# One decoder layer: experts' rows each written to a place of their own and summed at the end, the last expert added on chip, per-layer work moved among the experts

## The chip, the cores and the metric

The program runs on one core of a Trainium2 chip. The metric is the device time of one execution in microseconds: the median of three runs of the kernel before is 1594.79 us (1594.51 to 1595.72). The profile shows one further execution. PE is the matrix engine, PEld its weight load, DVE, ACT and POOL the vector, scalar and general engines, SP the engine that here only issues DMAs.

## The reference, cut to what matters

One layer for 512 tokens of width 1024. Token mixing comes first (attention and a recurrent branch, merged and projected); it is untouched but for one set of stores. Then 32 experts, each token going to its best four, and last a gated per-layer input:

```python
xn = rmsnorm(h, norm_moe_g)
# per token: 4 of 32 experts, weights = softmax of the 4 best router logits
y_rows = (((clip(up) + 1) * swiglu(gate)) @ w_down[e] + b_down[e]) * weight
h = h + segment_sum(y_rows, token)          # four rows per token are added
pl_gate = sigmoid(rmsnorm(h, norm_pl_g) @ w_pl_gate + b_pl_gate)
pl = rmsnorm(p @ w_pl_proj, norm_pl_post_g)
out = rmsnorm(h + pl_gate * pl, norm_final_g)
```

Each expert has 12 MB of weights: `w_gate_up` 1024 x 2048 and `w_down` 1024 x 1024, in fp32. There are 2048 rows of results (512 tokens times 4) for 32 experts, 64 on average.

## The kernel before

**Weights.** All weights of the experts come through a ring of 20 buffers of 1 MB (`load_raw`, L622): eight of gate and up, four of down for each expert, 384 in all, issued by SP in that order. A buffer is loaded again as soon as PE has used it, so SP runs ahead of PE until it is short of buffers. Each hardware DMA uses one of eight semaphores in turn, so eight are outstanding.

**An expert.** The sorted order `ORDER` begins with two experts of the heavy class; then a light and a heavy one alternate, and the last two (numbers 30 and 31, counted from 0) are light. A heavy expert has room for 96 rows (three groups of 32), a light one for 64 (two). For each expert PE multiplies the gathered tokens with the eight gate-and-up buffers (`gate_up`, L924, an fp32 product for each group and quarter of the columns; four products on four column groups of the array run side by side, and each leaves two records in the trace), ACT and DVE apply the gating, and PE multiplies with the four down buffers (`down`, L974). ACT copies the result from PSUM with the row's weight (`h_t<-y,gate`).

**Adding up.** `scatter_add` (L893) adds the rows to the residual `h_dram` in HBM by an indirect DMA with an add, issued by POOL: 128 pieces of 512 numbers for the first 64 rows, and for a heavy expert 128 pieces of 256 numbers for the other 32. Places of an expert without a token go to rows of padding behind the 512 of `h_dram`. Each scatter waits for the one before.

**The end.** After the 384 weight buffers SP loads the per-layer projection `wpr`, the input `p` (`pt`) and the gate matrix (`pgr`). During the last expert PE transposes `pt` (L1067), after it PE computes the projection (`pp`, L1081 ff.; three products on rounded halves of the numbers, L70 to L72), and ACT and DVE split the gate matrix into halves (`pgh`, `pgl`). A branch (`tc.If`, L1094) follows that would compute further rows if an expert had more tokens than places; then `h_dram` is read back (`ht`, L1153). For each block of 128 tokens PE transposes `ht` (L1175) and multiplies with the gate matrix (`pg`, 48 products of 128x512), and DVE and ACT apply sigmoid, product, sum and the last norm.

Every engine works through its own list of instructions in order; the program's scheduler sets that list when the kernel is built, so a piece of code may stand earlier or later than in the text.

Of the kernel before, what the change touches and what calls it, by code (L numbers as in the profile page):

```python
# [20 lines left out]
P = 128  # L21
S = 512
# [20 lines left out]
def hybrid_block(  # L43
# [57 lines left out]
    mul2 = const.tile([P, 2], F32, name="mul2")  # L101
    off2 = const.tile([P, 2], F32, name="off2")
    pad2 = const.tile([P, 2], F32, name="pad2")
    for i, (n, m, s0) in enumerate(((64, 2, 0), (32, 4, 64))):
        part = const.tile([P, 2], I32, name=f"part{i}")
        nc.vector.tensor_single_scalar(part[:, 0:1], iota_p, n.bit_length() - 1, op=OP.logical_shift_right)
        nc.vector.tensor_single_scalar(part[:, 1:2], iota_p, n - 1, op=OP.bitwise_and)
        nc.vector.memset(mul2[:, i:i + 1], float(m))
        nc.vector.tensor_copy(off2[:, i:i + 1], part[:, 0:1])
        nc.vector.tensor_scalar(pad2[:, i:i + 1], part[:, 1:2], float(S + s0), float(m), op0=OP.add, op1=OP.mult)  # L110
    nc.vector.tensor_tensor(pad2, pad2, off2, op=OP.add)
# [28 lines left out]
    vals = route.tile([P, NTB, E, 5], BF16, name="vals")  # L140
# [6 lines left out]
    nc.vector.tensor_copy(vals[:, :, :, 3:], vidx.unsqueeze(2).to_broadcast([P, NTB, E, 2]))  # L147


    h_dram = dram.tile([S + CAP, D], F32, name="h_dram")  # L150
# [3 lines left out]
    vl_dram = dram.tile([P, E, NTB * 5], BF16, name="vl_dram")  # L154
# [10 lines left out]
    with ExitStack() as mix:  # L165
# [205 lines left out]
        with tc.tile_pool(name="s2", bufs=1) as s2, tc.tile_pool(name="p2", bufs=4, space=PSUM, reuse_waits="tile") as p2:  # L371
# [212 lines left out]
    LATE, NPL = 12 * E, 6  # L584

    def slot_of(n):
        return (n if n < LATE else n + NPL) % RING
# [6 lines left out]
    def raw_tile(n):  # L594
        return ring_tile(slot_of(n), [P, 2048], F32, f"raw{n}")
# [61 lines left out]
    def slot_rows(pool, psum, pe, vl, n=2):  # L657
# [3 lines left out]
        for i in range(n):  # L661
# [3 lines left out]
            for tb in range(NTB):  # L665
                nc.tensor.matmul(ip[:, i, :5], pes[i][:, tb], vl[:, tb], start=tb == 0, stop=tb == NTB - 1)
        iv = pool.tile([P, 2, 5], F32, name="ivg", bufs=2)[:, :n]
        act(iv, ip[:, :n, :5], AF.Copy)
# [5 lines left out]
        nc.vector.scalar_tensor_tensor(row, row, float(BIG), mul2[:, :n], op0=OP.add, op1=OP.mult)  # L674
        nc.vector.tensor_tensor(row, row, off2[:, :n], op=OP.add)
        dst = [pool.tile([P, 1], I32, name=f"dst{i}", bufs=2) for i in range(n)]
        for i in range(n):
            nc.vector.tensor_tensor(dst[i], row[:, i:i + 1], pad2[:, i:i + 1], op=OP.min)
# [6 lines left out]
    with ExitStack() as ep:  # L685
# [175 lines left out]
        for tb in range(NTB):  # L861
# [3 lines left out]
            nc.vector.tensor_reduce(gt[:, tb], oh.rearrange("q k e -> q e k"), axis=AX.X, op=OP.add)  # L865
    pjx.close()
# [5 lines left out]
    xpad = xp.tile([P, 128], F32, name="xpad")  # L872
# [16 lines left out]
    last_v = []  # L889
# [42 lines left out]
    def swiglu(psum, g, gu, aT):  # L932
# [6 lines left out]
        last_v.append(nc.vector.scalar_tensor_tensor(sg, sg, F7, u1, op0=OP.min, op1=OP.mult).ins)  # L939
# [12 lines left out]
    def down(psum, raws, aT, selcol, gate, y, rest, once=True, n=2):  # L952
# [19 lines left out]
        for i, k in order:  # L972
# [288 lines left out]
```

## Time and profile before

| | us |
|---|---|
| median of 3 runs | 1594.79 |
| profiled execution | 1593.8 |
| its span | 1592.2 |
| PE busy in the span | 1499.1 (94%) |
| DVE, ACT, POOL busy | 480.8, 422.8, 130.9 |
| share of the DMA engines: queue q1 (weights) | 71.8% |
| share of the DMA engines: queue q0 (POOL's DMAs) | 5.8% |

The experts take the stretch from 457 us to 1512 us. In the 40 slices of the page the DMA row reads 9 from slice 13 to slice 37 and the rate stands near 400 GB/s there; before it the DMA engines are mostly idle, and in the last three slices as well. A busy PE is not a PE at its peak: its share is read together with what it waits for.

### The profile page before, as it was taken

To read this page: it belongs to the slowest core of one execution; us is meant where nothing else is said; L and a number is where in the kernel's file an instruction comes from. 1 tells how busy PE (TensorE), PEld (TensorE's weight loads), DVE (VectorE), ACT (ScalarE), POOL (GpSimd) and SP (SyncE) were. 2 spreads that over 40 slices of the span, in tenths; PEclk is the share of its full clock that TensorE was granted. 3 is DMA by queue.
4 is the path that set the end of the run, shared out by engine and by line. 5 is a ranking of instruction groups with operands and counts; after the bars stand their busy time and mean duration, and the time that the engine had idled before them with its cause. 6 is when DMAs were issued, how large, how long until landed. Compare 5 with 4: busy or idle time off the path is not lost. (4 is left out here: it accounts for less than half of the span.)

```text
span 1592.2 us, 28449 instructions
## 1 busy us (share of the span) xinstructions
PE 1499.1 (94%) x11938; PEld 798.0 (50%) x11938; DVE 480.8 (30%) x1161; ACT 422.8 (27%) x764; POOL 130.9 (8%) x134
## 2 busy tenths in 40 slices
PE   7999999999999999999999999989999999999677
PEld 6888787777844343433434434334233332433256
DVE  7776655557432111211111111111121111210146
ACT  6878325555121110110111101011010110110167
POOL 1000000000001111101111011010110101101000
PEclk9999999999999999999999999999999999999889
DMA  7332431216788999999999999999999999999721
GB/s 221 98 106 80 123 102 54 80 57 235 288 344 328 371 395 401 398 393 392 397 400 390 396 402 396 392 393 399 401 396 402 389 397 403 398 400 398 310 80 53
DMA packets 105912, 479.99 MB, mean 301 GB/s; under 512 B 9857, under 2 KB 43353, under 8 KB 56016
## 3 DMA queue, kind: packets, MB, share of 16 engines
q1 hardware_dynamic: 93056, 450.97, 71.8%
q0 software_dynamic: 10448, 20.68, 5.8%
q10 hardware_dynamic: 2272, 6.45, 1.3%
q8 instruction: 95, 1.56, 0.4%
q14 instruction: 41, 0.34, 0.1%
HBM read 462.89 MB, written 17.17 MB: 302 GB/s over the span
## 5 line engine op out<-in xcount | busy, mean ns | idle before, releaser
L924 PE MATMUL gu<-raw,xa 128*32 128x512 f32 x5120 | 591.6, 594 | 24.6 <-DMA raw<-in_w_gate_up_dram 23.8
L924 PEld LDWEIGHTS gu<-raw,xa 128*32 128x32 f32 x5120 | 203.6, 110 | 364.9 <-issue 220.4
L974 PE MATMUL y<-raw,xa 128*32 128x512 f32 (+1 forms) x3072 | 316.7, 523 | 4.2 <-DMA raw<-in_w_down_dram 1.9
L937 DVE TENSOR_TENSOR sgu<-sgu,gu 128x256 f32<-128x256 f32 x48 | 20.2, 422 | 861.7 <-ACT sgu L62 861.7
L974 PEld LDWEIGHTS y<-raw,xa 128*32 128x32 f32 x3072 | 107.1, 109 | 158.0 <-issue 117.3
L62 ACT ACTIVATE sgu<-gu 128x256 f32<-128x256 f32 x48 | 18.4, 383 | 542.4 <-PE gu L924 542.4
L893 POOL DMA_INDIRECT h_dram<-h_t,dst x48 | 75.9, 1582 | 437.9 <-ACT h_t L62 298.4
L62 ACT ACTIVATE h_t<-y,gate 128x512 f32<-128x512 f32 (+1 forms) x48 | 29.6, 616 | 225.9 <-PE y L974 225.9
L62 ACT ACTIVATE whi<-wr 128x1024 fp32r<-128x1024 f32 x48 | 50.7, 1058 | 67.5 <-PE pj L71 36.8
L66 DVE TENSOR_TENSOR wlo<-wr,whi 128x1024 fp32r<-128x1024 f32 x47 | 57.2, 1219 | 26.0 <-ACT whi L62 25.7
L62 ACT ACTIVATE xa<-tpa 128x256 f32<-128x256 f32 x80 | 30.6, 383 | 123.0 <-PE tpa L947 99.3
L653 POOL TENSOR_SCALAR tok<-iv 64x1 int32<-64x1 f32 (+1 forms) x31 | 14.3, 461 | 500.6 <-ACT iv L62 500.6
L70 PE MATMUL pj<-xnh,whi 128*128 128x512 f32 x128 | 51.5, 403 | 0.0
L71 PE MATMUL pj<-xnl,whi 128*128 128x512 f32 x128 | 50.7, 396 | 0.0
L72 PE MATMUL pj<-xnh,wlo 128*128 128x512 f32 x128 | 50.2, 392 | 0.0
L917 PE MATMUL gu<-bias,eyep 96*32 96x512 bf16 x296 | 43.3, 384 | 5.6 <-DVE sgu L938 5.6
L62 ACT ACT_TABLE_LOAD x30 | 38.5, 1283 | 2.4 <-DVE lg L792 1.9
L636 POOL DMA_INDIRECT h_t<-xg_dram,tok x31 | 32.7, 1056 | 13.4 <-POOL tok L653 8.8
L947 PEld LDWEIGHTS tpa<-ident,sgu 128*128 128x128 f32 x96 | 15.1, 207 | 36.7 <-DVE sgu L939 23.3
L967 PE MATMUL y<-bias,eyep 96*32 96x512 bf16 (+1 forms) x176 | 20.1, 348 | 11.5 <-ACT h_t L62 11.5
L903 PE MATMUL tpx<-ident,h_t 64*128 64x64 f32 (+1 forms) x248 | 29.8, 245 | 0.8
L70 PE MATMUL pg<-pgh,hT 128*128 128x512 f32 (+1 forms) x72 | 26.9, 374 | 0.2 <-ACT hT L62 0.2
(366 smaller groups left out, 1954.4 us busy)
## 6 DMA issues: line engine op xcount, KB each, us to landing
raw<-in_w_gate_up_dram SPq DMA_DIRECT2D x256, 1024.0 KB, 22.0
raw<-in_w_down_dram SPq DMA_DIRECT2D x128, 1024.0 KB, 22.0
wr<-in_w_in_dram SPq DMA_DIRECT2D x12, 1024.0 KB, 5.3
wr<-in_w_merge_dram SPq DMA_DIRECT2D x8, 1024.0 KB, 5.5
wr<-in_w_lru_out_dram SPq DMA_DIRECT2D x4, 1024.0 KB, 5.1
wo<-in_w_out_dram SPq DMA_DIRECT2D x4, 1024.0 KB, 5.3
pgr<-in_w_pl_gate_dram SPq DMA_DIRECT2D x4, 1024.0 KB
xt<-in_x_dram SPq DMA_DIRECT2D x4, 512.0 KB, 6.1
```

The source lines that it names most:

```text
L62: return nc.scalar.activation(out_, in_, func, **kw).ins
L66: return eng.tensor_tensor(lo, src, hi.bitcast(F32), op=OP.subtract).ins
L70: nc.tensor.matmul(o, lh, rh, start=first, stop=False)
L71: nc.tensor.matmul(o, lh, rl, start=False, stop=False)
L72: nc.tensor.matmul(o, ll, rh, start=False, stop=last)
L636: return nc.gpsimd.indirect_dma_start(out=xr, out_offset=None, in_=xg_dram[:, :], in_offset=bass.IndirectOffsetOnAxis(ap=tok[:, 0:1], axis=0),
L893: nc.gpsimd.indirect_dma_start(out=h_dram.rearrange("r (c n) -> (r c) n", n=n), out_offset=bass.IndirectOffsetOnAxis(ap=dst[i][:, 0:1], ax ...
L903: nc.tensor.transpose(tp[:, j], xr[:cap, (j2 + j) * P:(j2 + j + 1) * P], ident[:cap, :cap])
L917: nc.tensor.matmul(gs[g][32 * j:32 * j + 32], selcol.to_broadcast([3 * E, 32]), src, start=True, stop=False)
L924: mm = nc.tensor.matmul(gs[g][32 * j:32 * j + 32], xT[:, k, 32 * g:32 * g + 32], src[:, :, 256 * j:256 * j + 256], start=False, stop=k == ...
L937: nc.vector.tensor_tensor(sg, sg, gp, op=OP.mult)
L974: mm = nc.tensor.matmul(o, aT[:, g, k % 2, k // 2], raws[k // 2][:, k % 2 * D + cs.start:k % 2 * D + cs.stop], start=False, stop=k == KT - ...
```

## The change

- **A place for each row.** A new tensor `y_dram` has four rows for each token. The column of the expert among the token's four (`kt`, carried as a sixth number in `vals`) gives the place, so no two rows meet, and `put` writes without an add. An expert's place without a token gets an index out of bounds and is dropped. `y_dram` is filled with zeros first: 16 stores of 0.5 MB on SP's queue, where one store of padding stood on ACT's.
- **Summing.** For each block of 128 tokens the four rows are read back (`planes`, two DMAs of 1 MB), and POOL (one) and DVE (three) add them to `h`.
- **The last expert** (number 31) isn't written: PE multiplies the one-hot matrix of its tokens with its result (`hp`, an fp32 product for each half of the columns) and DVE adds that.
- **Moved.** The projection's loads stand before expert 28's weights (two slots of the ring are kept for its result from there on), its product behind expert 28 (one fp32 product, `pl_product`, where three products of halves stood), its norm behind expert 29. The branch and the loads of the gate matrix, of the first block's rows and of `h` stand between the gate-and-up and the down buffers of expert 31; the split of the gate matrix stands within expert 31.

```diff
+    h_dram = dram.tile([S, D], F32, name="h_dram")
+
+    y_dram = dram.tile([S * TOPK, D], F32, name="y_dram")
...
+            zt = s2.tile([P, D], F32, name="zt")
             nc.gpsimd.memset(zt, 0.0)
-            nc.scalar.dma_start(h_dram[S:], zt)
+            for r in range(S * TOPK // P):
+                nc.sync.dma_start(y_dram[r * P:r * P + P], zt)
...
+    LATE, KEPT = 12 * (E - 4), 2
+    at_slot, turn = [], 0
+    for n in range(12 * E):
+        if n == LATE:
+            wpr_at, plt_at = turn % RING, [(turn + 1 + i) % RING for i in range(KEPT)]
+            turn += 1 + KEPT
+        while n >= LATE and turn % RING in plt_at:
+            turn += 1
+        at_slot.append(turn % RING)
+        turn += 1
...
+        nc.vector.tensor_scalar(row, row, float(BIG), float(TOPK), op0=OP.add, op1=OP.mult)
+        nc.vector.tensor_tensor(row, row, iv[:, :, 5], op=OP.add)
...
-    def scatter_add(y, dst):
+
+    def put(y, dst):
         for i, (a, n) in enumerate(((0, 512), (512, 256))[:len(dst)]):
             nc.gpsimd.indirect_dma_start(
-                out=h_dram.rearrange("r (c n) -> (r c) n", n=n),
+                out=y_dram.rearrange("r (c n) -> (r c) n", n=n),
                 out_offset=bass.IndirectOffsetOnAxis(ap=dst[i][:, 0:1], axis=0),
-                in_=y[:, a:a + n], in_offset=None, bounds_check=(S + CAP) * (D // n) - 1, oob_is_err=True,
-                compute_op=OP.add)
+                in_=y[:, a:a + n], in_offset=None, bounds_check=S * TOPK * (D // n) - 1, oob_is_err=False)
...
+        def load_rows(tb):
+
+            pr = [ring_tile(k, [P, 2, D], F32, "planes") for k in (DN[:2] if tb % 2 else FREE[4:])]
+            for i in range(2):
+                nc.sync.dma_start(pr[i], yv[tb * P:tb * P + P, 2 * i:2 * i + 2])
+            return pr
...
+        def tail_loads():
+
+            pgr = [ring_tile(k, [P, 2, D], F32, "pgr") for k in FREE[:4]]
+            for i in range(4):
+                nc.sync.dma_start(pgr[i], w_pl_gate[0].rearrange("(q i j) n -> i q j n", i=4, j=2)[i])
+            pr = [load_rows(0)]
+            h2 = [ring_tile(k, [P, 2, D], F32, "h2") for k in GU[:2]]
+            for i in range(2):
+                nc.sync.dma_start(h2[i], h_dram[i * 2 * P:(i + 1) * 2 * P].rearrange("(b t) d -> t b d", b=2))
+            return pgr, pr, h2
...
+        def pl_loads():
+
...
+            plts = [ring_tile(k, [P, 2, D], F32, "plt") for k in plt_at]
+            nc.sync.dma_start(wpr, w_pl_proj[0].rearrange("(k q) n -> q k n", q=P))
+            nc.sync.dma_start(pt, p[0, 0].rearrange("(b q) n -> q b n", q=P))
+            nc.sync.dma_start(gpl, norm_pl_g[0].rearrange("(q j) -> q j", j=KT))
...
+            for tb in range(NTB):
+                for n in range(2):
+                    ns = slice(n * 512, n * 512 + 512)
+                    pp = p_t.tile([P, 512], F32, name="pp7", tag="tp")
+                    for k in range(2):
+                        nc.tensor.matmul(pp, pT[:, tb, k], wpr[:, k, ns], start=k == 0, stop=k == 1)
+                    act(plts[tb // 2][:, tb % 2, ns], pp, AF.Copy)
+                    act(pp, pp, AF.Square, accum_out=sq[:, tb, n:n + 1])
+            return sq
...
+            if 12 * e == LATE:
+                wpr, pt, pT, gpl, plts = pl_loads()
+            raws = [load_raw(12 * e + t) for t in range(8)]
+            if e + 1 == E:
+                past()
+                pgr, pr, h2 = tail_loads()
+            raws += [load_raw(12 * e + t) for t in range(8, 12)]
...
+            else:
+
+                identb = fp.tile([P, P], BF16, name="identb", tag="pe")
+                nc.vector.tensor_copy(identb, ident)
+                tp = p_t.tile([P, S], F32, name="tpo", tag="tp")
+                for tb in range(NTB):
+                    nc.tensor.matmul(tp[:, tb * P:tb * P + P], pes[0][:, tb], identb, start=True, stop=True)
+                ohT = ob[:, 1, :S]
+                act(ohT, tp, AF.Copy)
+                whs, wls = tail_split()
...
-            split(wph[:, k], wpl[:, k], wpr[:, k])
-        for i in range(4):
...
+            if e + 1 < E:
+                put(y, dst)
+            if 12 * e == LATE:
+                sq = pl_product()
+            if 12 * e == LATE + 12:
+                ob = pl_norm()
...
+        def add_rows(tb, pr):
+            nc.gpsimd.tensor_tensor(pr[1][:, 0], pr[1][:, 0], pr[1][:, 1], op=OP.add)
+            nc.vector.tensor_tensor(pr[0][:, 0], pr[0][:, 0], pr[0][:, 1], op=OP.add)
+            nc.vector.tensor_tensor(ht[tb], ht[tb], pr[0][:, 0], op=OP.add)
+            nc.vector.tensor_tensor(ht[tb], ht[tb], pr[1][:, 0], op=OP.add)
+
+        def add_last(tb):
+
+            for c in range(2):
+                hp = ptl.tile([P, 512], F32, name="hp")
+                nc.tensor.matmul(hp, ohT[64 * c:64 * c + 64, tb * P:tb * P + P], y[64 * c:64 * c + 64, :512], start=True, stop=True)
+                nc.vector.tensor_tensor(ht[tb][:, c * 512:c * 512 + 512], ht[tb][:, c * 512:c * 512 + 512], hp, op=OP.add)
...
+        pr.append(load_rows(1))
+        add_rows(0, pr[0])
+        add_last(0)
...
         transpose_h(0)
         for tb in range(NTB):
-            act(junk, plt[tb], AF.Square, accum_out=sums[:, NTB + tb:NTB + tb + 1])
-        rsl = inv_rms(sums[:, NTB:])
-        for tb in range(NTB):
-            nc.vector.scalar_tensor_tensor(plt[tb], plt[tb], rsl[:, tb:tb + 1], gpo, op0=OP.mult, op1=OP.mult)
-        for tb in range(NTB):
             if tb + 1 < NTB:
+                add_rows(tb + 1, pr[tb + 1])
+                add_last(tb + 1)
+                if tb + 2 < NTB and tb + 2 == len(pr):
+                    pr.append(load_rows(tb + 2))
```

SP's list at the end of the experts, before (`raw_11570` is the last buffer of expert 31; a semaphore DMAHW is that of a load from SP, DMASW of a DMA from POOL):

```order
L622 DMA raw_11568<-in_w_down_dram 128x2048 [waits DMAHW2_49,PE_49]
L622 ISA
L622 DMA raw_11570<-in_w_down_dram 128x2048 [waits DMAHW3_49,PE_49]
L1038 DMA wpr<-in_w_pl_proj_dram 128x2x1024 [waits DMAHW4_49,PE_49]
L1039 DMA pt<-in_p_dram 128x4x256 [waits DMAHW5_49,PE_49]
L1044 DMA pgr_11578<-in_w_pl_gate_dram 128x2048 [waits DMAHW6_49,PE_49]
```

And after, from the last gate-and-up buffer of expert 31 over the branch; `raw_13335` is its first down buffer:

```order
L1101 DMA pgr<-in_w_pl_gate_dram 128x2048 [waits DMASW4_49,DMASW5_49,DMASW3_49,DMASW6_49,DMASW2_49,DMASW7_49,DMASW1_49,DMAHW2_49,DMASW0_49,PE_49]
L1101 DMA pgr<-in_w_pl_gate_dram 128x2048 [waits DMAHW3_49,DVE_49,Activation_49]
L1101 DMA pgr<-in_w_pl_gate_dram 128x2048 [waits DMASW7_49,DMAHW4_49,DMASW0_49,Activation_49]
L1101 DMA pgr<-in_w_pl_gate_dram 128x2048 [waits DMAHW5_49]
L1094 DMA planes<-y_dram 128x2048 [waits DMAHW6_49]
L1094 DMA planes<-y_dram 128x2048 [waits DMAHW7_49]
L1105 DMA h_13331<-h_dram 128x2x1024 [waits DMAHW0_49,PE_49]
L1105 DMA h_13332<-h_dram 128x2x1024 [waits DMAHW1_49,PE_49]
L626 ISA
L626 DMA raw_13335<-in_w_down_dram 128x2048 [waits DMAHW2_49]
```

Eight loads of 1 MB now stand ahead of the last four weight buffers, and the first of them waits for all of POOL's DMAs, the `put` of expert 30 among them.

PE's list at the end of expert 28 (a light expert; `y` is its down product, `gu` the next expert's gate and up) after the change; before, none of the rows `tpp` and `pp` stood here:

```order
L1141 MATMUL tpp<-ident,ptx 128x128 x4
L1148 MATMUL pp_11125<-wpr,ptx 128x512
L983 MATMUL y_11063<-raw_10930,xa 32x512 x8
L1148 MATMUL pp_11125<-wpr,ptx 128x512
L1148 MATMUL pp_11130<-wpr,ptx 128x512
L983 MATMUL y_11063<-raw_10932,xa 32x512 x8
L1148 MATMUL pp_11130<-wpr,ptx 128x512
L1148 MATMUL pp_11135<-wpr,ptx 128x512 x2
L1148 MATMUL pp_11140<-wpr,ptx 128x512 x2
L1148 MATMUL pp_11145<-wpr,ptx 128x512 x2
```

All 16 products of the projection and its eight transpositions stand between the down buffers of expert 28 and the next expert.

PE's list from expert 31's last down buffer on, before (`pp` is the projection):

```order
L974 MATMUL y_11723<-raw_11568,xa 32x512 x8
L974 MATMUL y_11723<-raw_11570,xa 32x512 x8
L72 MATMUL pp_11790<-wph,pT 128x512
L70 MATMUL pp_11798<-wph,pT 128x512
L71 MATMUL pp_11798<-wpl,pT 128x512
L72 MATMUL pp_11798<-wph,pT 128x512
```

And after:

```order
L983 MATMUL y_13478<-raw_13339,xa 32x512 x8
L983 MATMUL y_13478<-raw_13341,xa 32x512 x8
L1220 MATMUL hp<-h_t_3055,ob 128x512 x3
L1249 MATMUL tp_13551<-ident,h_13331 128x128 x4
L1249 MATMUL tp_13558<-ident,h_13331 128x128 x4
L1220 MATMUL hp<-h_t_3055,ob 128x512
L70 MATMUL pg_13602<-pgh,hT_13548 128x512
```

Behind the last down buffer PE now has the four `hp` of the first two blocks and eight transpositions before the gate product `pg`; the projection, the branch and the read of `h_dram` are gone from there.

## Rows read from the trace of the kernel before

**Rows 1.** Busy time by stretch: engines, granted clock, share of the DMA engines, rate.
```profile
680.00:932.60 252.60, 246.18 (x2360) 101.32 (x2360) 36.03 (x140) 28.11 (x76) 31.29 (x28) 1.00 1.02 396
932.60:1468.20 535.60, 500.26 (x4708) 190.03 (x4708) 71.05 (x277) 55.92 (x151) 60.81 (x54) 1.00 1.02 397
1535.20:1583.80 48.60, 48.38 (x240) 41.22 (x240) 31.90 (x57) 42.17 (x70) 0.00 (x0) 0.97 0.09 33
1583.80:1592.20 8.40, 0.00 (x0) 0.00 (x0) 2.95 (x10) 3.60 (x8) 0.00 (x0) 0.64 0.17 62
```
**Rows 2.** Longest wait of PE, first from 680 to 932.6, then from 932.6 to 1468.
```profile
PE y L967 <- ACT h_t L62: 3.4, 4, 0.8
...
PE gu L924 <- DMA raw<-in_w_gate_up_dram: 19.8, 31, 1.7
```
**Rows 3.** ACT's copy of experts' results (light experts): start, duration, instruction.
```profile
869.51 0.69 ACT L62 ACTIVATE h_t<-y,gate 128x512 f32<-128x512 f32 x1 [7.23 <-PE y L974]
...
932.64 0.69 ACT L62 ACTIVATE h_t<-y,gate 128x512 f32<-128x512 f32 x1 [7.23 <-PE y L974]
...
1402.93 0.69 ACT L62 ACTIVATE h_t<-y,gate 128x512 f32<-128x512 f32 x1 [9.37 <-PE y L974]
...
1468.24 0.69 ACT L62 ACTIVATE h_t<-y,gate 128x512 f32<-128x512 f32 x1 [7.23 <-PE y L974]
```
**Rows 4.** DMA queue q0, 1470 to 1479 us, one scatter of 256 KB: packets, MB, share.
```profile
q0 software_dynamic: 144, 0.26, 15.8%
```
**Rows 5.** DMA queue q0, 1450 to 1460 us, one scatter of 128 KB.
```profile
q0 software_dynamic: 144, 0.13, 8.2%
```
**Rows 6.** DMA queue q1, 1566 to 1574 us, two stores of the output, 256 KB each.
```profile
q1 hardware_dynamic: 288, 0.52, 17.7%
```
**Rows 7.** DMA issues of the whole run: count, KB each, median us to landing.
```profile
wr<-in_w_in_dram SPq DMA_DIRECT2D x12, 1024.0 KB, 5.3
...
h_dram<-h_t,dst POOLq DMA_INDIRECT x48, 9.1
```
**Rows 8.** DMA issues, 1513 to 1520 us: the last scatter, with little other traffic.
```profile
h_dram<-h_t,dst POOLq DMA_INDIRECT x1, 5.0
```
**Rows 9.** Timeline, expert 30's gate and up at the pace of its loads.
```profile
1449.84 1.92 PE L924 MATMUL gu<-raw,xa 128*32 128x512 f32 x16 [0.50 <-DMA raw<-in_w_gate_up_dram]
...
1452.34 1.92 PE L924 MATMUL gu<-raw,xa 128*32 128x512 f32 x16 [0.58 <-DMA raw<-in_w_gate_up_dram]
```
**Rows 10.** Timeline from the last expert's down product to the first gate product.
```profile
1500.57 1.54 PE L1067 MATMUL tpp<-ident,pt 128*128 128x128 f32 x6 [9.09 <-DMA pt<-in_p_dram]
...
1504.87 7.07 PE L974 MATMUL y<-raw,xa 128*32 128x512 f32 x62
...
1512.04 0.69 ACT L62 ACTIVATE h_t<-y,gate 128x512 f32<-128x512 f32 x1 [7.45 <-PE y L974]
1512.62 8.41 ACT L62 ACTIVATE pgh<-pgr,gpl 128x1024 fp32r<-128x1024 f32 x8
1513.19 1.57 POOL L893 DMA_INDIRECT h_dram<-h_t,dst  x1 [42.44 <-ACT h_t L62]
...
1535.22 0.80 PE L70 MATMUL pg<-pgh,hT 128*128 128x512 f32 x1 [0.24 <-ACT hT L62]
```
**Rows 11.** Chain of waits in order of time: one gate product in the dense stretch.
```profile
1560.14 0.23 PE pg L71
```
**Rows 12.** Groups by line: mean duration of passes over 128x1024 fp32.
```profile
L66 DVE TENSOR_TENSOR wlo<-wr,whi 128x1024 fp32r<-128x1024 f32 x47 | 57.2, 1219 | 26.0 <-ACT whi L62 25.7
...
L66 POOL TENSOR_TENSOR wlo<-wr,whi 128x1024 fp32r<-128x1024 f32 x1 | 2.4, 2387 | 13.2 <-ACT whi L62 13.2
...
L1196 DVE SCALAR_TENSOR_TENSOR plt<-plt,rs,rows 128x1024 f32<-128x1024 f32 x4 | 4.9, 1281 | 0.0
```
**Rows 13.** DMA queue q10, 180 to 200 us: stores of padding and loads of biases.
```profile
q10 hardware_dynamic: 160, 0.52, 8.2%
```
**Rows 14.** ACT, rounding of the projection `v`, first and second piece.
```profile
198.61 1.15 ACT L62 ACTIVATE vwh<-wr 128x512 fp32r<-128x512 f32 x2 [4.38 <-PE yp L71]
204.05 1.16 ACT L62 ACTIVATE vwh<-wr 128x512 fp32r<-128x512 f32 x2 [4.29 <-PE yp L71]
```

More of the change, by code (lines that the diff above doesn't have):

```diff
@@ L98, in hybrid_block @@
     nc.gpsimd.iota(iota_p, pattern=[[0, 1]], base=0, channel_multiplier=1)
-    mul2 = const.tile([P, 2], F32, name="mul2")
     off2 = const.tile([P, 2], F32, name="off2")
[L103 to L111, printed above, removed]
+    for i, n in enumerate((64, 32)):
+        part = const.tile([P, 1], I32, name=f"part{i}")
+        nc.vector.tensor_single_scalar(part, iota_p, n.bit_length() - 1, op=OP.logical_shift_right)
+        nc.vector.tensor_copy(off2[:, i:i + 1], part)
     trib = const.tile([P, P], BF16, name="trib")
@@ new lines, in tail_split @@
+        def tail_split():
+            whs = [ring_tile(k, [P, 2, D], F32R, "pgh") for k in GU[4:]]
+            wls = []
+            for i in range(4):
+                wls.append(ring_tile([GU[2], *FREE][i], [P, 2, D], F32R, "pgl"))
+                for j in range(2):
+                    gc = gpl[:, 2 * i + j:2 * i + j + 1]
+                    act(whs[i][:, j], pgr[i][:, j], AF.Copy, scale=gc)
+                    nc.vector.scalar_tensor_tensor(wls[i][:, j], pgr[i][:, j], gc, whs[i][:, j].bitcast(F32),
+                                                   op0=OP.mult, op1=OP.subtract)
+            return whs, wls
@@ new lines, in pl_norm @@
+        def pl_norm():
+            ob = r1.tile([P, 2, D], F32, name="ob", tag="a8b")
+            nc.sync.dma_start(ob[:, 0], norm_pl_post_g[0:1].to_broadcast([P, D]))
+            rsl = fp.tile([P, NTB], F32, name="rsl")
+            nc.vector.tensor_tensor(rsl, sq[:, :, 0], sq[:, :, 1], op=OP.add)
+            act(rsl, rsl, AF.Sqrt, scale=1.0 / D, bias=eps)
+            nc.vector.reciprocal(rsl, rsl)
+            for tb in range(NTB):
+                pl = plts[tb // 2][:, tb % 2]
+                nc.vector.scalar_tensor_tensor(pl, pl, rsl[:, tb:tb + 1], ob[:, 0], op0=OP.mult, op1=OP.mult)
+            return ob
@@ L1083, in hybrid_block @@
-        for tb in range(NTB):
-            for n in range(2):
-                ns = slice(n * 512, n * 512 + 512)
-                pp = p_gu.tile([P, 512], F32, name="pp7", tag=f"gu{(2 * tb + n) % G}")
-                for k in range(2):
-                    mm3(pp, (pT[:, tb, 0, k], pT[:, tb, 1, k]), (wph[:, k, ns], wpl[:, k, ns]),
-                        first=k == 0, last=k == 1)
-                act(plts[tb // 2][:, tb % 2, ns], pp, AF.Copy)
-    cnt = nc.values_load(cm_i[0:1, 0:1], min_val=0, max_val=S)
@@ L1146, in hybrid_block @@
+            down(p_y, raws[8:], aT, sel, gate, y, rest, n=n)
+            if e + 1 < E:
+                put(y, dst)
+            if 12 * e == LATE:
+                sq = pl_product()
+            if 12 * e == LATE + 12:
+                ob = pl_norm()
+            if e + 2 == E:
+                nc.vector.tensor_copy(cm_i, cmax)
     with tc.tile_pool(name="tl", bufs=2, reuse_waits="tile") as tl, \
             tc.tile_pool(name="ptl", bufs=2, space=PSUM, reuse_waits="tile") as ptl:
-        rows = [spare(n, [P, 2, D], F32, f"rows{n}") for n in (17, 18)]
```

213 lines of the change are left out of this document (92 added, 121 removed).

## The prediction

> **What bounds the kernel now.** I read the stretches of the page first, then the waits of PE, then the times at which experts' results are copied, and last the timeline of the end. In the experts' stretch the share of the DMA engines is 1.02 from 680 to 1468 us, at 396 to 397 GB/s [rows 1]: it is full all the time. PE is not always short of data, though. From 680 to 932.6 us it never waits for a weight buffer, from 932.6 on it does [rows 2]. The copies of light experts show the same: one pair (a heavy and a light expert) takes 63.13 us early (869.51 to 932.64), and 535.6 / 8 = 66.95 us later (932.64 to 1468.24, eight pairs) [rows 3]. So 63.1 us per pair is PE's own pace, 66.95 that of the transfers, and PE lives on a full ring until about 935 us. From there the experts end when the transfers do. Behind them comes a serial end: PE waits 9 us for `pt`, finishes expert 31, its result is copied at 1512.04, and the first gate product starts at 1535.22, 23.2 us later, with 8.41 us of ACT's splitting in between [rows 10]. Then PE is busy 48.38 of 48.6 us, and 8.4 us follow without PE [rows 1].
>
> **Scatter without add.** One add of 256 KB takes 0.158 x 9 = 1.42 us of all DMA engines [rows 4], one of 128 KB 0.082 x 10 = 0.82 us [rows 5]. There are 48 [rows 7]: 32 of the first kind and 16 of the second (heavy experts), 32 x 1.42 + 16 x 0.82 = 58.6 us. What a plain write costs is shown by the output: two stores of 256 KB in the same 2 KB packets take 0.177 x 8 = 1.42 us, so 0.71 us each, half [rows 6]. That gives 31 x 0.71 + 16 x 0.41 = 28.6 us, and if places without a token cost nothing (2048 rows in 32 x 64 + 16 x 32 = 2560 places), 0.8 times that, 22.9 us. Saved: 30 to 36 us; I take 33. The bounds are 36 and nothing (a write in the crowd costs what an add does), and I lean on the output's row because its packets are of the same size.
>
> 33 us over 16 pairs is 2.1 per pair, 66.95 - 2.1 = 64.9 us: nearly PE's pace. By transfers the copy of expert 28 (1402.93 before) comes at 1402.93 - 33 x 28/32 + 3.8 = 1377.8, where 3.8 us are the 1.5 MB of `wpr` and `pt` now ahead of it at 2.5 us per MB (two waits for a buffer lie 2.50 us apart [rows 9]). By PE it comes at 932.64 + 7 x 63.13 = 1374.6. I take 1378, so from here PE sets the pace.
>
> **Zero stores.** Eight MB on SP's queue ahead of the second load for `v`. In the stores of the padding 0.52 MB took 0.082 x 20 = 1.64 us of all engines [rows 13], so 8.4 MB take 26 us from about 174 us, and the load behind them lands near 206 instead of before 199. Its rounding is due at 199, PE wants the result at about 204 [rows 14]. Cost 0 to 8 us, I take 2, since PE has the group before to work on. Everything later shifts: 1380. The routing's few added passes lie beside PE's products and cost nothing here; without that cover, some 4 us.
>
> **Projection behind expert 28.** 16 fp32 products of 128x512. Sixteen records of the experts' product take 1.92 us, four column groups side by side, two records to a product [rows 9], so a product on the full array takes 0.86 us here by estimate, and 16 take 13.8; eight transpositions (six in 1.54 us when cold, L1067 [rows 10]) about 0.9. Together 14.7 us of PE. The lower bound is 16 x 0.23 = 3.7 [rows 11]; I take the upper, as these are not split into halves. PE has just caught up with the transfers, so nothing hides it: expert 30 is one pair later, 1380 + 14.7 + 63.1 = 1457.8.
>
> **The new wait.** SP's first `pgr` load waits for the `put` of expert 30, and behind it stand all four `pgr`, two `planes`, two `h` and the last four down buffers: 12 MB. POOL issues the `put` about 1.1 us behind the copy (1513.19 against 1512.04 [rows 10]); it lands 5.0 us after that when quiet [rows 8], 9.1 in the crowd [rows 7]. I take 7, since the loads of expert 31's gate and up end by then: 1466. In this gap of some 7 us the transfers have nothing to do. The first MB lands 5.3 us after issue from a quiet queue [rows 7], eleven more follow at 2.5: 1466 + 5.3 + 27.5 = 1498.8. Expert 31's gate and up (13.7 us of PE), the split of `pgr` and the adding of the first rows lie in that time and cost nothing; the branch too.
>
> **The end.** The last buffer takes 1.9 us of PE, the copy 0.8: 1501.5, against 1512.73 before. Then two `hp`, an add, a third `hp` before the transpositions, these, their copy and the fourth: two products of 0.86, 0.8 for the add, then 2 for transpositions and copy, in all 4.6: the first gate product starts at 1506.1 instead of 1535.2. The dense stretch of 48.6 grows by four more `hp` (3.4) and 1 us of small waits, then 8.4 follow: 1506.1 + 48.6 + 3.4 + 1 + 8.4 = 1567.5. The profiled execution took 1593.8 at a span of 1592.2, so 1.6 lie around it: 1569.1, 24.7 below its own time. The median of the runs is 1.0 above the profiled one: **1570 us**.
>
> In that end DVE does 31.90 + 2.95 - 4.9 = 30 us for four blocks [rows 1, 12], 7.5 each. Added are three passes of 1.22 and two of half that, 4.9: 12.4 us per block, against PE's 48 x 0.23 + 0.9 + 1.7 = 13.6. PE stays ahead by about a us.
>
> **Rivals.**
> - *DVE sets the end.* POOL's added pass takes 2.39 us where DVE's takes 1.22 [rows 12], and no row shows both at once on 1024 columns. If DVE stands still for POOL's three passes in the dense stretch, its block takes 14.8 instead of 12.4 and is longer than PE's: 3 x 1.2 + 2.4 for the first block's start, 6 us, 1576. For: the margin is one us. Against: DVE can begin block 0 before PE. The Trainium skill (GPSIMD Engine Reference, section 1, Specifications) says that the two engines share their interfaces to SBUF and that DVE's instructions with two SBUF inputs contend, which speaks for this rival; no run here shows it yet.
> - *PE's time for the projection is partly hidden*, the `put` lands in 5 us and the zeros cost nothing: 4 + 2 + 2 less and small waits gone, near 1560; with the projection wholly hidden, 1555. For: if transfers are slower than I think, PE has waits to fill behind expert 28, and its products stand between two down buffers. Against: then the saving is smaller as well.
> - *No gain.* A write in the crowd costs nearly what an add costs, saving 8 instead of 33 us: 25 x 28/32 = 22 later, 1592. Most of the shortened end is then paid for by the 8 MB now ahead of the last weights. For: reads and writes share the engines, and the output's row is from a quiet stretch. Against: the adds were read in the crowd and cost twice as much at the same size.
> - *Slower.* The mechanism is the same price, further on: `put` pieces of 2 KB and 1 KB, each to a row of its own, cost as much as the adds or more. Saving nothing puts expert 30 at 1457.8 + 29, and the 12 MB queue behind its `put`: 1599. It decides from a price of 1.4 us for 256 KB at all places, or 1.75 if empty places are free. The stores of the output [rows 6] speak against it.
>
> A rule that would help and not hurt: the Trainium skill (Runtime: NRT & Kernel Launch, section Instruction fetch mechanics) says a taken branch whose target lies outside the current pages stalls its engine for the fetch. The branch left PE's path at the end for a place where PE waits anyway; by that rule a few us of the 23.2 go with it, and they are already in my sum, which counts the new end from its own parts.
>
> **How the numbers follow.** Forecast (1562 to 1582) 0.58, DVE sets the end 0.14 (mostly inside that range's upper part), hidden projection 0.12, no gain 0.09, slower 0.07. A difference of 0.2% (3 us) is what a measurement of this kernel tells from none. Of the case without gain a third each falls faster, within and slower: faster 0.87, within 0.2% 0.04, slower 0.09. Range 1553 to 1590: from the hidden projection with the saving of 36, to the forecast with a saving of about 12 (21 x 28/32 = 18 later). The likeliest one's own range is 1562 to 1582; cases of the other sign hold little.
>
> **What would show it.** Right: pairs of experts at 63 to 65 us up to expert 28; no wait of PE for weights before 1300 us; a pair behind expert 28 with about 15 us of `pp`; DMA engines idle for 5 to 10 us around 1460, ended by the `put`; the last down buffer near 1499; first `pg` within 8 us of it; `pg` dense for 52 us. A scatter of 256 KB at 0.5 to 0.75 us of all engines. Wrong: pairs still at 67 us (the price of a write), PE waiting for DVE's `hT` or adds in the dense stretch by more than 3 us, a gap in PE near 204 us above 4, or an end of the experts that comes 15 us later than 1499.

## The result, and the profile after

The changed kernel takes 1578.64 us (median of four runs, 1577.56 to 1579.38) where the one before takes 1595.09 in the same series: a ratio of 0.9896, interval 0.9879 to 0.9913. It is 16.5 us faster; I had forecast 1570, 24.8 faster. The profiled execution has a span of 1576.6 us.

Busy time by stretch of the changed kernel (PE, PEld, DVE, ACT, POOL, then the granted clock, the share of the DMA engines and GB/s); the first and the last line answer to those of [rows 1]:

```profile
680.00:932.60 252.60, 246.20 (x2364) 101.02 (x2360) 35.91 (x140) 28.11 (x76) 24.51 (x28) 1.00 1.02 407
932.60:1314.80 382.20, 371.90 (x3562) 151.05 (x3555) 53.87 (x210) 42.17 (x114) 36.77 (x42) 1.00 1.01 404
1380.00:1420.00 40.00, 40.00 (x261) 13.09 (x258) 3.46 (x10) 14.27 (x31) 1.02 (x1) 1.00 0.71 276
...
1418.00:1504.40 86.40, 65.37 (x604) 21.28 (x594) 28.52 (x57) 15.91 (x30) 7.76 (x6) 0.88 1.01 411
1512.80:1568.90 56.10, 53.03 (x249) 42.37 (x248) 44.08 (x65) 34.33 (x58) 7.41 (x3) 0.94 0.23 86
```

The third line is new: from 1380 to 1420 us the DMA engines move 276 GB/s instead of about 410 while PE is busy all the time. Before that they are full and after it they are full again, to the last weight buffer.

ACT's copies of light experts, as in [rows 3], and of the last expert:

```profile
935.08 0.69 ACT L62 ACTIVATE h_t<-y,gate 128x512 f32<-128x512 f32 x1 [7.23 <-PE y L983]
...
1314.82 0.69 ACT L62 ACTIVATE h_t<-y,gate 128x512 f32<-128x512 f32 x1 [7.23 <-PE y L983]
...
1387.37 0.69 ACT L62 ACTIVATE h_t<-y,gate 128x512 f32<-128x512 f32 x1 [1.55 <-PE y L983]
...
1459.78 0.69 ACT L62 ACTIVATE h_t<-y,gate 128x512 f32<-128x512 f32 x1 [7.23 <-PE y L983]
...
1506.95 0.69 ACT L62 ACTIVATE h_t<-y,gate 128x512 f32<-128x512 f32 x1 [19.28 <-PE y L983]
```

Six pairs from 935.08 to 1314.82 are 63.29 us each: PE's pace now holds to 1314 us, where it gave way to the transfers' 66.95 at 933 before. The two pairs that share the projection take 72.55 and 72.41.

The loads' queue `q1` and POOL's queue `q0` from 935 to 1315 us (packets, MB, time as a share of 16 engines), with SP's issues of weight buffers in that stretch (behind the x their number; the kernel before also shows the median us to landing), first in the kernel before, then after the change:

```profile
q1 hardware_dynamic: 19737, 143.72, 93.5%
q0 software_dynamic: 3520, 6.59, 8.0%
...
raw<-in_w_gate_up_dram SPq DMA_DIRECT2D x89, 1024.0 KB, 22.4
raw<-in_w_down_dram SPq DMA_DIRECT2D x47, 1024.0 KB, 23.1
```

```profile
q1 hardware_dynamic: 20231, 147.31, 96.2%
q0 software_dynamic: 2400, 6.06, 4.7%
...
raw<-in_w_gate_up_dram SPq DMA_DIRECT2D x95, 1024.0 KB
raw<-in_w_down_dram SPq DMA_DIRECT2D x44, 1024.0 KB
```

In 380 us POOL's queue takes 30.4 us for 5.7 pairs before and 17.9 for 6.0 after: 5.4 and 3.0 us per pair. The loads move 2.5% more, so their own pace is now 66.95 x 143.72 / 147.31 = 65.3 us per pair, by estimate. That is slower than PE's 63.29: SP issued 139 weight buffers while PE used the 144 of six pairs. PE drew on the lead that the full ring had given it, and at expert 28 it had to wait for six buffers (PE's waits from 1310 to 1390 us, the first row):

```profile
PE gu L933 <- DMA raw<-in_w_gate_up_dram: 4.1, 6, 0.9
```

One `put` of up to 256 KB, that of expert 30, from 1460 to 1472 us:

```profile
q0 software_dynamic: 80, 0.22, 4.7%
```

It took 0.047 x 12 = 0.56 us of all DMA engines, where an add took 1.42 [rows 4].

What SP waits for from 1370 to 1480 us in the changed kernel (total, times, longest):

```profile
SPq L626 <- PE pp L1148: 23.5, 1, 23.5
...
SPq L1101 <- DMA h_t<-xg_dram,tok: 11.5, 1, 11.5
```

The first wait is one load of expert weights whose slot of the ring still holds `wpr`: it can only go once the last product of the projection has read it. While SP stands there the transfers run dry. The second is the wait of the first `pgr` load for POOL's DMAs; the `put` of expert 30, issued at 1460.74, landed 8.2 us later, at 1468.9, and the load went out at 1471.12. The row names one of POOL's gathers as the last to release it, and what held it for those last 2 us is open.

The timeline of the end, from the last expert's down product to the first gate product, answers to [rows 10]:

```profile
1497.46 6.90 PE L983 MATMUL y<-raw,xa 128*32 128x512 f32 x48 [12.88 <-DMA raw<-in_w_down_dram]
1504.96 1.92 PE L983 MATMUL y<-raw,xa 128*32 128x512 f32 x16 [0.60 <-DMA raw<-in_w_down_dram]
...
1507.69 1.13 PE L1220 MATMUL hp<-h_t,ob 64*128 64x512 f32 x4 [0.81 <-ACT h_t L62]
...
1510.65 1.16 PE L1249 MATMUL tp<-ident,h 128*128 128x128 f32 x8
...
1512.79 0.50 PE L70 MATMUL pg<-pgh,hT 128*128 128x512 f32 x1
```

From copy to first gate product it is 5.8 us instead of 23.2. But the rest, 48.6 + 8.4 us before, is 63.8 now (1512.8 to 1576.6), and in it PE waits once for DVE:

```profile
PE tp L1249 <- DVE h L1221: 3.1, 1, 3.1
```

DVE and POOL just ahead of that wait; each stretched pass of DVE lies beside one of POOL (L1211):

```profile
1512.58 2.40 POOL L1211 TENSOR_TENSOR planes<-planes 128x1024 f32<-128x1024 f32 x1 [19.24 <-DMA planes<-y_dram]
1513.24 2.82 DVE L1213 TENSOR_TENSOR h<-h,planes 128x1024 f32<-128x1024 f32 x1
...
1517.52 2.38 POOL L1211 TENSOR_TENSOR planes<-planes 128x1024 f32<-128x1024 f32 x1 [2.54 <-DMA planes<-y_dram]
1518.61 2.38 DVE L1212 TENSOR_TENSOR planes<-planes 128x1024 f32<-128x1024 f32 x1
1522.77 1.21 DVE L1213 TENSOR_TENSOR h<-h,planes 128x1024 f32<-128x1024 f32 x1
...
1524.67 2.85 POOL L1211 TENSOR_TENSOR planes<-planes 128x1024 f32<-128x1024 f32 x1 [4.77 <-DMA planes<-y_dram]
1525.21 2.87 DVE L1291 TENSOR_TENSOR gs<-gs,plt 128x512 f32<-128x512 f32 x1
```

PE's clock around that wait, in the changed kernel (columns as above):

```profile
1525.00:1530.00 5.00, 4.37 (x18) 2.66 (x17) 5.00 (x6) 0.35 (x2) 2.53 (x1) 1.00 0.00 0
1530.00:1532.40 2.40, 0.00 (x0) 0.00 (x0) 2.40 (x6) 2.37 (x4) 0.00 (x0) 0.77 0.00 0
1532.40:1538.40 6.00, 5.95 (x19) 5.02 (x20) 5.27 (x7) 5.04 (x10) 0.00 (x0) 0.52 0.00 0
```

After the 3.1 us without work the granted clock is 0.52 for 6 us, which is nearly all at the lower of the two levels, 1.2 GHz: some 3 us more are lost than the wait itself.

### The profile page after: what moved, and what is told of

Read it like the earlier page. It is cut to its first block, busy times and chain, and to the rows that moved or that the text cites. A ratio compares the mean times of both kernels' runs of the same rounds, so it can differ in the third digit from the quotient of the medians.

```text
span 1576.6 us, 28522 instructions
## 1 busy us (share of the span) xinstructions
PE 1503.3 (95%) x11954; PEld 802.8 (51%) x11954; DVE 506.8 (32%) x1188; ACT 420.3 (27%) x766; POOL 113.7 (7%) x137
## 5 line engine op out<-in xcount | busy, mean ns | idle before, releaser
L933 PE MATMUL gu<-raw,xa 128*32 128x512 f32 x5120 | 585.1, 594 | 5.0 <-DMA raw<-in_w_gate_up_dram 4.9
L933 PEld LDWEIGHTS gu<-raw,xa 128*32 128x32 f32 x5120 | 210.7, 110 | 328.3 <-issue 222.9
L903 POOL DMA_INDIRECT y_dram<-h_t,dst x47 | 47.4, 1009 | 372.7 <-ACT h_t L62 258.4
L657 POOL TENSOR_SCALAR tok<-iv 64x1 int32<-64x1 f32 (+1 forms) x31 | 14.7, 475 | 541.5 <-ACT iv L62 541.5
```

The source lines that it names most:

```text
L903: nc.gpsimd.indirect_dma_start(out=y_dram.rearrange("r (c n) -> (r c) n", n=n), out_offset=bass.IndirectOffsetOnAxis(ap=dst[i][:, 0:1], ax ...
L933: mm = nc.tensor.matmul(gs[g][32 * j:32 * j + 32], xT[:, k, 32 * g:32 * g + 32], src[:, :, 256 * j:256 * j + 256], start=False, stop=k == ...
```

## The experiments

Each was timed against the kernel before on the same chip. Medians of the kernel before were 1594.4 to 1595.4 us in the four series. Runs of one kernel spread by 2 to 6 us, so two variants that differ by less than 3 us are not told apart.

| run | median us | ratio to before, interval |
|---|---|---|
| changed kernel | 1578.64 | 0.9896, 0.9879 to 0.9913 |
| 1 slot of `wpr` skipped | 1576.04 | 0.9877, 0.9860 to 0.9893 |
| 2 no wait for the put | 1576.80 | 0.9881, 0.9865 to 0.9898 |
| 3 both | 1570.05 | 0.9837, 0.9821 to 0.9854 |
| 4 put adds | 1597.41 | 1.0014, 1.0004 to 1.0024 |
| 5 half the projection | 1572.30 | 0.9851, 0.9835 to 0.9868 |
| 6 POOL's pass on DVE | 1573.14 | 0.9866, 0.9850 to 0.9883 |
| 7 other order of the end | 1571.56 | 0.9849, 0.9832 to 0.9865 |
| 8 the same, pass on DVE | 1571.71 | 0.9858, 0.9841 to 0.9874 |
| 9 = 3 with 6 | 1565.25 | 0.9820, 0.9806 to 0.9835 |
| 10 = 8, loads reordered | 1569.73 | 0.9841, 0.9826 to 0.9856 |
| 11 = 10 with idle products | 1564.87 | 0.9812, 0.9797 to 0.9827 |
| 12 zeros from POOL | 1578.11 | 0.9897, 0.9880 to 0.9915 |

**1. The slot of `wpr` is skipped for one round.**

```diff
+            again = turn + RING
             turn += 1 + KEPT
-        while n >= LATE and turn % RING in plt_at:
+        while n >= LATE and (turn % RING in plt_at or turn == again):
```

> The buffer that first follows round the ring onto the slot of wpr is put into the next slot, so that no load waits for the projection's last product; the slot is used again a round later. Theory A (lost transfers): in the changed kernel SP stands 23.5 us for that slot, the DMA engines move 11.05 instead of about 16.5 MB from 1380 to 1420 us (13 us lost), and from 1419 us on they are full to the last down buffer. The 23.5 us go here and the engines stay full from 1380 to 1440; but the first pgr load still waits for the put of expert 30 (about 1470), so a new idle stretch of 6 to 10 us opens before it: last down buffer 1500 to 1504, 1575 to 1579 us in all. Theory B (my forecast: only the put's wait counts): last down buffer at 1504, no change, 1578 to 1579, and no idle stretch before 1470 that was not there. Theory C (neither: PE sets the end): no change and PE's wait before the last down product unchanged at 12.9 us.

Measured: SP's wait of 23.5 us is gone and the engines stay full, but the idle time comes back ahead of the put (share 0.30 from 1460 to 1470):

```profile
1380.00:1420.00 40.00, 40.00 (x264) 12.89 (x262) 2.98 (x9) 14.65 (x32) 1.02 (x1) 1.00 1.01 412
1460.00:1470.00 10.00, 10.00 (x96) 3.07 (x92) 0.00 (x0) 0.00 (x0) 0.61 (x1) 1.00 0.30 97
```

Theory A's place and size are right. In the profiled execution, the fastest of the four, the last expert is copied at 1502.42, 4.5 us earlier; the 2.6 us by the medians are by themselves within the spread.

**2. The first `pgr` loads don't wait for the put** (the branch's buffers move to other slots).

```diff
-                oxa = ring_tile(FREE[1], [P, 2, KT * CAP], F32, "oxa")
+                oxa = ring_tile(FREE[4], [P, 2, KT * CAP], F32, "oxa")
...
-                oyx = ring_tile(FREE[2], [P, 2, D], F32, "oyx")
+                oyx = ring_tile(FREE[5], [P, 2, D], F32, "oyx")
...
-                                    r = ring_tile(FREE[0], [P, 2048], F32, "oraw")
+                                    r = ring_tile(FREE[3], [P, 2048], F32, "oraw")
```

> The untaken branch's three buffers take other slots of the ring, so that the first three pgr loads no longer wait for the put of expert 30 (and the gathers) but only for PE; pgr's last load and the planes still do. Theory A: the engines were full at that time anyway; last down buffer still at 1504, 1577 to 1579 us. Theory B: SP's 11.5 us there go, the last down buffer lands 5 to 8 us earlier, 1571 to 1574 us.

Measured: the first `pgr` goes out at 1459.49 instead of 1471.12, and the last expert is copied at 1506.94 against 1506.95, the first gate product at 1512.78 against 1512.79. The edit frees three of the twelve loads; the fourth still waits 8.6 us for POOL's DMAs. But the engines' share is 1.01 from 1460 to 1480 us, so nothing was left there to be gained by sending a load earlier. Theory B, the forecast's, falls as the sole cause.

**3. Both.**

> Both edits. Theory A: 13 us of transfers come back and no wait takes their place: last down buffer at 1490 to 1494, first gate product about 1500, 1564 to 1568 us. Theory B: as with the second edit alone, 1571 to 1574. Theory C: 1577 to 1579.

Measured: the last expert's copy 6.5 us earlier (1500.43), first gate product 1506.26, 8.6 us by the medians, with an interval clear of the changed kernel's. The direction is A's, and more than B's, but short of 13 us: pgr's fourth load still waits for POOL's DMAs (14.9 us), and the engines' share is 0.68 from 1460 to 1470. Two limits lie one upon the other here: by the last expert's copy the first edit alone brings 4.5 us, the second nothing, both 6.5; by the medians 2.6, 1.8 and 8.6.

**4. The put adds again.**

```diff
-                in_=y[:, a:a + n], in_offset=None, bounds_check=S * TOPK * (D // n) - 1, oob_is_err=False)
+                in_=y[:, a:a + n], in_offset=None, bounds_check=S * TOPK * (D // n) - 1, oob_is_err=False, compute_op=OP.add)
```

> The scatter adds again, into the zeros of its own place (the result is the same): only the price of the scatter comes back. My price (1.42 us of all engines for 256 KB with the add, 0.7 without; 2.1 us per pair of experts): pairs at 66 to 67 us from 935 on instead of 63.3, expert 28's copy at about 1408 instead of 1387, and since the transfers then have no idle stretch behind it the whole is 1592 to 1600 us. Rival (the write costs nearly what an add does, the gain came from the shorter end alone): pairs within 0.5 us of 63.3, 1577 to 1582 us.

Measured: 18.8 us slower than the changed kernel, even slower than before by 0.04 to 0.24%. Pairs take 66.36 us (933.75 to 1331.90 in six), expert 28 is copied at 1405.39. So the write without an add carries the whole gain; at an add's price all other edits together cost 2 us. From 935 to 1315 us:

```profile
q1 hardware_dynamic: 19841, 144.50, 94.4%
q0 software_dynamic: 3520, 5.84, 7.0%
```

The loads move 1.9% less than in the changed kernel, 1.3 us per pair, and POOL's queue takes 1.7 us per pair more (7.0% of 66.36 against 4.7% of 63.29). The 3.1 us between the pairs are more than either, because 63.29 is PE's pace, while in run 4 PE waits 13.7 us for weights in those six pairs.

**5. Half of the projection left out.**

```diff
-                    for k in range(2):
-                        nc.tensor.matmul(pp, pT[:, tb, k], wpr[:, k, ns], start=k == 0, stop=k == 1)
+                    for k in range(1):
+                        nc.tensor.matmul(pp, pT[:, tb, k], wpr[:, k, ns], start=True, stop=True)
```

> The changed kernel with 8 of the 16 products of the projection left out (the half of each sum over k=1); loads, slots and transpositions stay. My step (nothing hides PE's time for the projection): expert 28 to 30 takes 65 instead of 72.4 us, SP's wait for the slot of wpr falls from 23.5 to about 16 us, and the end comes 6 to 8 us earlier: 1569 to 1573. Theory A (lost transfers) expects the same size, by 7 us less of idle DMA engines. Rival (PE's time there is hidden by data it would wait for anyway): 1576 to 1579.

Measured: expert 28 to 30 takes 65.98 us, SP's wait at the slot 16.7, the time falls by 6.3 us. PE's time there is not hidden, though this run alone doesn't tell it from SP's shorter wait, which theory A expects to give as much. Run 3 does: no load waits for the slot there, the engines are full from 1380 to 1420 us (share 1.02), and the two experts still take 72.42 us.

**6. POOL's pass on DVE.**

```diff
-            nc.gpsimd.tensor_tensor(pr[1][:, 0], pr[1][:, 0], pr[1][:, 1], op=OP.add)
+            nc.vector.tensor_tensor(pr[1][:, 0], pr[1][:, 0], pr[1][:, 1], op=OP.add)
```

> The changed kernel with the one added pass that POOL does moved to DVE. Theory D (DVE and POOL disturb each other): in the changed kernel three passes of DVE beside a POOL pass take 2.82, 2.38 and 2.87 us instead of 1.21, 1.21 and 0.68, 5 us in all, and PE waits 3.1 us for DVE's h; here every DVE pass takes its undisturbed time and PE's wait shrinks to under 1.5 us: 1574 to 1577. Rival (DVE simply has too much work, and POOL's help is worth its price): three more passes of 1.22 us on DVE, PE waits 4 to 6 us: 1579 to 1581.

Measured: 5.5 us faster, more than theory D allowed. DVE's passes over planes and `h` take 1.21 to 1.23 us throughout, PE waits for nothing behind its first gate product, and its clock stays up where it fell before:

```profile
1532.00:1538.00 6.00, 6.00 (x30) 4.95 (x29) 5.97 (x9) 4.33 (x7) 0.00 (x0) 1.00 0.01 3
```

The wait of 3.1 us and the slow 6 us behind it (about 3 lost) make up the gain.

**7 and 8. Another order of the end:** three `pgr` pieces, the down buffers, the planes, the last `pgr` piece, `h`; the planes are summed first. In 8 all adds are on DVE.

```diff
                 past()
-                pgr, pr, h2 = tail_loads()
+                pgr = [load_pg(i) for i in range(3)]
             raws += [load_raw(12 * e + t) for t in range(8, 12)]
+            if e + 1 == E:
+                pr, h2 = tail_loads()
...
-            nc.vector.tensor_tensor(ht[tb], ht[tb], pr[0][:, 0], op=OP.add)
-            nc.vector.tensor_tensor(ht[tb], ht[tb], pr[1][:, 0], op=OP.add)
+            nc.vector.tensor_tensor(pr[0][:, 0], pr[0][:, 0], pr[1][:, 0], op=OP.add)
```

> Both edits of the third run, and the loads of the end in another order: three pgr pieces, the four down buffers, then planes (which wait for the put), the last pgr piece and h; the planes are summed first and h is added last. Theory A: the engines stay full from 935 us to the last load, the last load (h) lands near 1492 instead of 1509, expert 31 is copied at 1488 to 1491, first gate product 1495 to 1500: 1558 to 1564 us. Rival (the end is set by the chain of adds behind the planes, which now come last): first gate product no earlier than in the third run (1506), 1567 to 1571 us.

> The same with POOL's pass on DVE. Theory D: 1 to 4 us less than with POOL, since four DVE passes are no longer stretched: 1555 to 1562. Rival: DVE is the longer engine in the gate's stretch and it is 1 to 4 us slower than with POOL.

Both misses. The engines are full to the last down buffer and the last expert is copied at 1493.79 and 1493.03, as theory A had it but for 3 us; the first gate product comes at 1501.96 and 1501.60. Yet the whole is no faster than run 3. In run 8 PE waits twice for DVE behind that product (2.3 and 1.3 us), since the second block's planes come late, and the clock falls:

```profile
1500.00:1505.00 5.00, 5.00 (x16) 4.06 (x16) 1.38 (x2) 3.77 (x6) 0.00 (x0) 0.52 0.88 341
1520.00:1530.00 10.00, 10.00 (x27) 6.71 (x26) 8.68 (x12) 5.04 (x10) 0.00 (x0) 0.57 0.31 105
```

**9. Runs 3 and 6 together.**

> The third run's kernel (no load waits for the projection's slot, the first pgr loads not for the put) with POOL's pass on DVE. If what the two edits gave (8 us) and what the sixth run gave (5.5 us) are separate places, they add: 1564 to 1567 us, first gate product at 1506, no wait of PE behind it and its granted clock 1.00 to the end of the gate products. If they are the same time counted twice: 1569 to 1572.

Measured: 1565.25. The two gains lie in different places and add, and POOL's pass on DVE gives 4.8 us here by the medians, as it gave 5.5 in run 6; from 1506 to 1557 us PE's clock is 1.00. Between the last expert and the first gate product PE stands for 0.8 us twice, and the clock stays up:

```profile
1500.00:1505.00 5.00, 3.45 (x15) 1.75 (x16) 2.51 (x3) 1.21 (x3) 0.00 (x0) 1.00 1.01 423
```

**10. Run 8 with the second block's planes loaded ahead of the second half of `h`.**

```diff
+        pr.append(load_rows(1))
         nc.sync.dma_start(bpg, b_pl_gate[0:1].to_broadcast([P, D]))
+        load_h(h2, 1)
         nc.sync.dma_start(gfin, norm_final_g.rearrange("(o d) -> o d", o=1).to_broadcast([P, D]))
-        pr.append(load_rows(1))
```

> The eighth run's kernel (tail in another order, adds on DVE) with the second block's planes and then b_pl_gate loaded ahead of the second half of h, and the split of the last pgr piece behind the first block's adds. In the eighth run the gate products began 11 us earlier than in the changed kernel, but PE waited twice for DVE (2.3 and 1.3 us), and its granted clock was 0.52 in 1500 to 1505 and 0.57 in 1520 to 1530, so that nothing was left. If the late planes of the second block and that clock took it: no wait of PE for DVE above 1 us, clock above 0.9 from the first gate product on, 1558 to 1565 us. Rival (DVE has more work per block than PE, whatever the order): PE waits at the later blocks instead, 1568 to 1572.

Measured: 1569.73. The time is the rival's, the mechanism is not: PE no longer waits for DVE behind the first gate product, but the clock is 0.50 from 1500 to 1505 all the same, after pauses of 0.8, 0.8 and 2.4 us between the last expert and that product.

**11. Run 10 with 16 products between, whose result is not used.**

```diff
+        warm = ptl.tile([P, 512], F32, name="pg7", bufs=4)
+        for i in range(16):
+            nc.tensor.matmul(warm, whs[0][:, 0, :P], whs[0][:, 0, :512], start=i == 0, stop=i == 15)
```

> The tenth run's kernel with 16 further products of 128x512 on PE (their result is not used) between the last expert's rows and the first block's transpositions, where PE stood for 0.8, 0.8 and 2.4 us and the granted clock then was 0.50 from 1500 to 1505 us. If PE's pauses there cost the clock: 0.9 or more from 1500 to 1505, and the end 2 to 4 us earlier than in the tenth run (1562 to 1568 us, and below 1563 in the profiled span), although PE does more. Rival (the clock falls for another reason, or the added products delay the transpositions): clock still near 0.5 there, time the same or 1 to 3 us more.

The same two stretches, first of run 10, then of run 11:

```profile
1495.00:1500.00 5.00, 1.98 (x5) 0.85 (x6) 4.69 (x5) 0.74 (x1) 0.00 (x0) 0.83 1.01 387
1500.00:1505.00 5.00, 5.00 (x16) 4.09 (x16) 2.51 (x3) 3.81 (x6) 0.00 (x0) 0.50 0.93 340
```

```profile
1495.00:1500.00 5.00, 5.00 (x22) 3.23 (x20) 4.23 (x5) 1.63 (x2) 0.00 (x0) 1.00 0.99 401
1500.00:1505.00 5.00, 4.73 (x25) 3.41 (x22) 3.01 (x4) 3.57 (x6) 0.00 (x0) 1.00 0.94 338
```

More work on PE, and the clock stays at 1.00: the pauses had cost it. How much time that gives is less sure: 4.9 us by the medians (1562.14 to 1567.34 against 1566.00 to 1570.86), but the two intervals touch, and the two profiled executions lie 1.1 us apart (1564.87 and 1566.00). In time it is level with run 9; both beat the kernel before by 1.8 to 1.9% and the changed one by 13 to 14 us.

**12. The zeros stored by POOL.**

```diff
-                nc.sync.dma_start(y_dram[r * P:r * P + P], zt)
+                nc.gpsimd.dma_start(y_dram[r * P:r * P + P], zt)
```

> The changed kernel with the 16 stores of zeros issued by POOL instead of SP. My step put 2 us on them, because SP's next load for v stands behind them. The traces say otherwise: v's first product starts at 204.0 in both kernels. If they cost nothing: v at 204 here too, the first expert's result no earlier than 495, and 1577 to 1580 us in all. If they cost what I put on them: 2 us earlier, 1575 to 1577, with the first expert's result near 494.5.

Measured: no difference, 1578.11. `v` starts at 204.1, 204.0 and 204.1 us before, after and here: the zero stores cost nothing.

## Why the prediction was right, and where not

The direction, the range and the largest cause held; the time was 8.6 us too low. In the profiled span it is 9.1 us, 1576.6 for 1567.5: 2.0 of them were there at expert 30's copy, 4.2 came between it and the last down buffer, 0.5 from there to the first gate product, and 2.4 behind that.

- **Scatter without add: right cause, a little oversized.** The price of one `put` was right: 0.56 us measured, 0.71 x 0.8 = 0.57 forecast. POOL's queue fell by 2.4 us per pair, but the loads' own pace only by about 1.6, to 65.3, where I took 2.1 off, to 64.9. The pairs of 63.29 hide this, since PE lived on the ring's lead. With 1.6 my own sum gives expert 28's copy at 1402.93 - 14 x 1.6 + 3.8 = 1384.3 for 1377.8.
- **Zero stores 2 us, routing 0: the wrong way round.** The first expert's result comes 1.5 to 3.4 us later in the changed kernel and its twelve variants (495.0 to 496.9 against 493.54), and run 12 shows that the zero stores have no part in it. The routing had no cover: putting the third array in order adds four transpositions and four small fp32 products on PE, 1.4 us. The rest, perhaps the one-hot passes on DVE, wasn't tested. The sum was right by luck.
- **The projection: right.** 15.7 us measured (14.43 of products, 1.26 of transpositions) for 14.7, and unhidden, by runs 3 and 5. About 4 of it stood ahead of expert 28's copy, which with the slower loads makes 1388 of the forecast 1380 (1387.4 measured); expert 30's came at 1459.8 for 1457.8.
- **The new wait: the step that failed.** I let the transfers go idle around 1460 for want of the put. They were full there; the idle time lay at 1380 to 1420, (410 - 276) x 40 us = 5.4 MB or 13 us of transfers, because I had followed the loads past `put` but not the ring past `wpr`: in order of slots, a slot read late holds up all of SP's queue. That the chain still gave nearly the right end was luck: it counted a wait that cost nothing by itself and missed the one above it (runs 1 to 3). `pgr` went out at 1471.1 for 1466, and PE had the last down buffer at 1505.0 for 1498.8.
- **The end: the rival came true beside the forecast.** I gave 0.14 to DVE standing still beside POOL, with 6 us; run 6 shows 5.5, and the sign that I had named for being wrong, a wait of PE for DVE of more than 3 us, is there with 3.1. "PE stays ahead by about a us" didn't allow for passes of 2.4 to 2.9 us. The rule that I cited from the Trainium skill (GPSIMD Engine Reference, section 1, Specifications) is borne out, and more sharply than I used it: the passes in question end 1.08, 1.09 and 0.56 us behind POOL's, little less than they take alone, so DVE stood until POOL was done. The Trainium skill (SBUF — State Buffer, section Who interferes with whom) says that whoever issues first holds the shared interface for the whole instruction in certain DVE modes and that the other blocks; the three ends fit that for adds too.
- **The slower rival had its price wrong and its sum right:** a `put` costs less than half of an add, but at an add's price the change is slower than before (run 4, 1597.4, where I had put 1599).
- **The branch.** PE still waits 3.4 us at it (1463.03), at a place where it later waits 12.9 us for weights, so it costs nothing, as the forecast took it. No run shows what that wait is made of.

What stays open: what held the first `pgr` load for 2 us after the put had landed, and what the later start of the experts is made of besides the 1.4 us of products. The granted clock from 440 to 460 us is 0.74 in the profiled execution and in run 5, 0.91 in run 8, and 0.83 before and in the other ten variants; those ten come 1.8 to 3.4 us later than before all the same, so the clock is not the main part.

## What to carry to other kernels

Follow every slot that a moved tile takes, not only its queue: in a ring issued in order, one buffer that is read late stops all loads behind it, and the loss shows as idle DMA engines 10 us later and on. A steady pace of results can be the engine's own while it uses up what was loaded ahead: compare the buffers loaded with those used before you call it the loads' pace. When removing one wait gains nothing, look for a second one just beneath it, and test both together. Near the end of a kernel, count a short pause of PE twice: once for itself and once for the lower clock behind it; two of 0.8 us alone cost no clock here (run 9).

## What the runs showed of the hardware

- An indirect write of rows without an add took 0.56 us of all DMA engines for one of up to 256 KB (0.22 MB moved), with an add 1.42 (0.26 MB). What POOL's queue gave up went to the loads: their share rose from 93.5% to 96.2% and their bytes from 143.72 to 147.31 MB in 380 us. No run shows a price of the add beyond the queue's own time.
- DVE passes with two inputs in SBUF don't overlap with a POOL pass of the same kind: 1.21 us became 2.82 and 2.38, 0.68 became 2.87. Two adds with one input in PSUM, beside the second POOL pass, took 1.29 us together, as they do without POOL.
- A pause of PE of 3.1 us in an otherwise dense stretch was followed by 6 us at a granted clock of 0.52; pauses of 0.8, 0.8 and 2.4 us by 5 us at 0.50. Two pauses of 0.8 us alone left it at 1.00. Products that nobody reads, put into the pauses, kept it at 1.00, and the kernel was 4.9 us faster by the medians, with intervals that touch.
